# The last quarter of an MLP's first product by seven half-size products instead of eight

## The chip, the cores and the metric

One core of a Trainium2 chip runs the kernel. The metric is the device time of one execution in microseconds. Unless a profile is meant, it is the median of several executions. Engines: PE is TensorE (matmul), PEld its weight load, DVE VectorE, ACT ScalarE, POOL GpSimd, SP SyncE, which here only issues DMAs.

## The reference

One layer of a decoder in float32: 512 tokens, model width 1024. Two mixers (gated linear attention, GLA, and latent attention, MLA) work on the same normalised stream and are merged by gates; an MLP with squared ReLU follows. Each sub-layer ends in a residual sum and a layer norm.

```python
D_MODEL, SEQ, D_FF = 1024, 512, 4096
def layer(x):                                    # (512, 1024), float32
    h  = layer_norm(x, ln_in)
    h1 = layer_norm(alpha * h + token_mixer(h), ln1)      # GLA + MLA, gates, output product
    a  = jnp.square(jax.nn.relu(h1 @ w_ff1))              # (512, 4096): the product in question
    return layer_norm(alpha * h1 + a @ w_ff2, ln2)
```

The change is in `h1 @ w_ff1`, in its last 1024 of 4096 columns, and in what makes its operands ready.

## The kernel before

**Products in three terms.** TensorE's fast float32 form keeps fewer bits than float32, so each operand is held as a high part (a rounded copy) and a low part (the difference), and each product is three matmuls into the same bank: high·high, high·low, low·high. For weights, ACT makes the high part (`whi<-wraw`, L185) and DVE the low part (`wlo<-wraw,whi`, L186). Both have two buffers.

**The stream of weights.** All weights go through one list, `stream`, of 512 KB items in the order of use. `pump(i)` is called ahead of item i. It issues SP's DMAs up to two items ahead (into `wraw`, three buffers) and splits one item ahead. An item whose weights are a sum has no DMA of its own; it takes its source from the table `WQ` (tiles `wq`), and a "post" function may form the next sum from a raw item.

**The MLP in four chunks** of 1024 hidden columns (`ci` 0 to 3). In each, the first product is plain (`gemm_fm`, L238 to L240): a 128x128 weight block stays, 512 tokens stream, 8 blocks of columns x 8 inner blocks x 3 terms = 192 matmuls of 128x512. Its evacuation `ev_h` takes the ReLU on ACT (L1296) and the square. In the first three chunks the second product is done by `win_f2` with seven products in place of eight (the scheme below, list `WIN`, L1268 to L1270), whose results are copied by ACT into `ev` tiles (L1280) and added to the tiles `res` by accumulating POOL DMAs (L1282). In the last chunk the hidden tile is made differently: ACT squares into the high part (L1310), POOL squares again (L1311), DVE takes the low part (L1312), and the second product is plain (`f2last`, L271 to L273 and L1343 to L1345).

**Seven products.** A product of 2 x 2 blocks takes eight block products; with sums of the operands (Strassen's scheme in Winograd's form) it takes seven. The kernel before uses it in `gemm_unit` for 1024 gate columns, under the key "g1" (L1016 to L1018). Weights are named by quadrant, "11", "12", "21", "22", and sums t1 = 11 + 12, t2 = t1 + 22, t3 = 12 + 22, t4 = t2 + 21. The order of the products is 11, 21, t1, 22, t2, t3, t4 (list `FMO`). The matching sums of the activations come from `op_sums` (L965 to L972, then a split, L112). The results of the seven products are joined on DVE (L1025, L1033, L1036). An item there is two inner blocks by 512 columns, so each operand has two items of 24 matmuls of 128x256.

**What sets the order.** Work beside the matmuls is written as generators that `tick` advances between matmuls (`spawn`, `finish`). The program's order is then settled for each engine by a scheduler that simulates the kernel with its own costs; `tc.issue_after` adds an edge that it must respect.

Of the kernel before, what the change touches and what calls it, by code (L numbers as in the profile page):

```python
# [10 lines left out]
F32 = mybir.dt.float32  # L11
# [8 lines left out]
P = 128  # L20
# [32 lines left out]
def tile_hybrid_block(ctx: ExitStack, tc: tile.TileContext, I, out, dbg=None):  # L53
# [86 lines left out]
    st = {"dma": 0, "spl": 0, "gates": ()}  # L140
    DMA_AHEAD, SPLIT_AHEAD = 2, 1

    def plan(name, c0, n, k_lo=0, k_hi=None, heads=None, res=False, per=2):
# [17 lines left out]

    def pump(i):
        while st["dma"] < min(len(stream), i + 1 + DMA_AHEAD):
# [10 lines left out]
            e["raw"] = raw  # L174
        while st["spl"] < min(len(stream), i + 2 + SPLIT_AHEAD):
            e = stream[st["spl"]]
            if st["spl"] > i + e.get("ahead", SPLIT_AHEAD) and not e["res"]:
                break
            nk, n = e["nk"], e["n"]
            hi, lo = [A([P, nk, T * 2 // nk], F32R, w) for w in HOME["a" if e["res"] else e.get("home", "w")]]  # L180
            raw = e["src"]() if "src" in e else e.pop("raw")
            with ExitStack() as gates:
                for g in st["gates"]:
                    gates.enter_context(tc.issue_after(g.ins))
                st["ins"] = act(hi[:, :nk, :n], raw[:, :nk, :n], AF.Copy)  # L185
                vtt(lo[:, :nk, :n], raw[:, :nk, :n], f(hi[:, :nk, :n]), op=ALU.subtract)  # L186
# [120 lines left out]
    FMO = (("11", 0), ("21", 1), ("t1", 2), ("22", 5), ("t2", 3), ("t3", 6), ("t4", 4))  # L307
    UNITS = {"g1": ("w_in", C_G + D)}

# [6 lines left out]

    def u_src(key, i, j, hf):
# [4 lines left out]
    def u_sum(key, a, to, hf, x):  # L322
        t = WQ[key, (to, hf)] = WQ[key, (a, hf)]
        vtt(t, t, x, op=ALU.add)


    for key in UNITS:
        PL[key] = []
        for op, _ in FMO:
            for hf in range(2):  # L330
                PL[key].append(len(stream))
                e = {"nk": 2, "n": T, "res": False}
                if op[0] != "t":
                    e["dmas"] = [(slice(0, 2), u_src(key, int(op[0]) - 1, int(op[1]) - 1, hf), None)]
                else:
                    e["src"] = lambda q=(key, (op, hf)): WQ[q]
                if op == "22":
                    e["post"] = lambda raw, q=(key, "t1", "t2", hf): u_sum(*q, raw)
                elif op == "t2":
                    e["post"] = lambda raw, q=(key, "t2", "t4", hf): u_sum(*q, WQ[key, ("21", q[3])])  # L340
                stream.append(e)
    plan_qr(0)
    PL["yg", 0] = plan("w_o_gla", 0, T)
# [25 lines left out]
    FC = 4  # L369
    F1 = [((0, 4), (4, 2), (6, 2))] + [tuple((b, 2) for b in range(0, 8, 2))] * 2 + [((0, 4), (4, 4))]  # L370
    WIN = (("11", 0, 0), ("21", 0, 1), ("11", 1, 0), ("21", 1, 1), ("T1", 0, 2), ("T1", 1, 2), ("T2", 0, 3), ("T2", 1, 3),
           ("T4", 0, 4), ("T4", 1, 4), ("22", 0, 5), ("22", 1, 5), ("T3", 0, 6), ("T3", 1, 6))
    fb = 0
    for ci in range(FC):
        nb = 8
        for b, w in F1[ci]:
            PL["f1", ci, b] = plan("w_ff1", (fb + b) * P, w * P, res=(ci == 0 and b == 0), per=8 // w)
        if ci < FC - 1:
            plan_src(("f2", ci), [(op, hf) for op, hf, _ in WIN], HOMES)
        else:  # L380
            plan_zip("f2last", [("w_ff2", 0, fb, True), ("w_ff2", T, fb, True)])
        fb += nb
# [601 lines left out]

    def u_load(key, op):
        for hf in range(2):
            t = WQ[key, (op, hf)] = A([P, 2, T], F32, "wq")
            nc.sync.dma_start(t, u_src(key, *{"21": (1, 0)}.get(op, (0, 1)), hf))
            if op != "21":
                nc.gpsimd.dma_start(t, u_src(key, *{"t1": (0, 0), "t3": (1, 1)}[op], hf), accum_op=ALU.add)  # L990

    def gemm_unit(key, ops, evac, after=None):

        bank, e1, e5, u2 = {}, {}, {}, {}
        nk = 2
        for n, (op, ph) in enumerate(FMO):
            items = PL[key][2 * n:2 * n + 2]
            for g in range(2):
                bk = ("a" if ph in (0, 3, 6, 4) else "b", g)
                opens = ph in (0, 2, 1)  # L1000
                if opens:
                    bank[bk] = (PX if ph == 1 else MM)()
                o = bank[bk]
                for hf, it in enumerate(items):
                    pump(it)
                    hi, lo = stream[it]["w"]
                    for pp in range(nk):
                        while len(ops) <= nk * hf + pp:
                            tick(3)
                        xh, xl = ops[nk * hf + pp][ph]  # L1010
                        for a in range(2):
                            c = slice((2 * g + a) * P, (2 * g + a + 1) * P)
                            oa = o[:, a * 256:(a + 1) * 256]
                            first = opens and hf == 0 and pp == 0 and a == 0
                            last = hf == 4 // nk - 1 and pp == nk - 1
                            mm(oa, hi[:, pp, c], xh, start=first, stop=False, skip_group_check=True)  # L1016
                            mm(oa, hi[:, pp, c], xl, start=False, stop=False, skip_group_check=True)  # L1017
                            mm(oa, lo[:, pp, c], xh, start=False, stop=last, skip_group_check=True)  # L1018
                        if pp % 2:
                            tick(3)  # L1020
                if ph == 0:
                    e1[g] = B([P, T], F32, "e1")
                    act(e1[g], o, AF.Copy)
                elif ph == 1:
                    vtt(e1[g], o, e1[g], op=ALU.add)  # L1025
                    evac(0, 0, g, e1[g], None)
                elif ph == 2:
                    e5[g] = B([P, T], F32, "e5")
                    act(e5[g], o, AF.Copy)
                elif ph == 3:  # L1030
                    u2[g] = B([P, T], F32, "u2")
                    act(u2[g], o, AF.Copy)
                    vtt(u2[g], bank["b", g], u2[g], op=ALU.subtract)  # L1033
                    evac(1, 0, g, u2[g], None)
                elif ph == 6:
                    vtt(e5[g], e5[g], o, op=ALU.subtract)  # L1036
                    evac(1, 1, g, e5[g], None)
                elif ph == 4:
                    evac(0, 1, g, o, None)
            if after:  # L1040
                after(op)


# [208 lines left out]
    def win_f2(ci, hid):  # L1252
        bank = {}
        for n, (op, hf, ph) in enumerate(WIN):
# [21 lines left out]
            if hf == 1:  # L1276
                for t in range(2):
                    o = bank[{3: 0, 6: 0, 5: 2}.get(ph, ph), t]
                    e = B([P, T], F32, "ev")
                    st["ev"] = act(e, o, AF.Copy, scale=-1.0 if ph == 4 else 1.0)  # L1280
                    for tt, j in (((0, 0),), ((0, 0),), ((2, 1),), ((0, 1),), ((2, 0),), ((0, 1),), ((2, 0), (2, 1)))[ph]:
                        nc.gpsimd.dma_start(res[tt + t][:, j * T:(j + 1) * T], e, accum_op=ALU.add)  # L1282
            if n == 9 and ci + 1 < FC - 1:
                win_load(ci + 1)

    WT = {}
    for ci in range(FC):
        nb = 8
# [5 lines left out]
        def ev_h(a, ps):  # L1294
            r = B([P, T], F32, "relu")
            act(r, ps, AF.Relu)  # L1296
            if win:
                if a % 2 == 0:
                    hid.append({"R": A([P, 2, T], F32, "hr")})
                ops = hid[-1]  # L1300
                R = ops["R"]
                act(R[:, a % 2, :], r, AF.Square)
                if a % 2:
                    h1 = A([P, 2, 2, 256], F32R, "h1p")
                    split(R[:, :, :256], h1[:, 0], h1[:, 1])
                    ops[0], ops[1] = [(h1[:, 0, i], h1[:, 1, i]) for i in range(2)]
                    spawn(win_hid(R, ops))
                return
            hh = A([P, 2, T], F32R, "hid0")
            act(hh[:, 0, :], r, AF.Square)  # L1310
            gtt(r, r, r, op=ALU.mult)  # L1311
            vtt(hh[:, 1, :], r, f(hh[:, 0, :]), op=ALU.subtract)  # L1312
            hid.append(hh)
        for b, w in F1[ci]:
# [14 lines left out]
        else:  # L1329
            bg, bb = bcast_row("ln2_g"), bcast_row("ln2_b")  # L1330
            gemm_tm(PL["f2last"], hid, T, ev_res, tts=(0, 1))
# [67 lines left out]
```

## Time and profile before

| | us |
|---|---|
| median of 3 runs (lowest to highest) | 901.56 (900.95 to 901.74) |
| the profiled execution, its own time | 901.97 |
| its span in the trace | 900.2 |
| mean granted TensorE clock, share of full speed | 0.998 |
| TensorE busy, of the span | 880.9 (98%) |
| VectorE busy | 585.5 (65%) |
| ScalarE busy | 427.3 (47%) |
| GpSimd busy | 178.0 (20%) |
| last chunk's first product, on TensorE | 805.03 to 848.54 |
| gate unit "g1", on TensorE | 274.32 to 317.94 |

Times inside the kernel are counted from the start of the span. A row of a timeline gives start, duration, engine, line, operation, output<-inputs, shape, and in brackets the idle time of the engine just before it with what ended it. A row of a group gives count | busy time, mean ns of one | idle time before them. A matmul's duration reaches over the start of the next ones, since they are pipelined; its cost in a dense stretch is the distance between starts.

### The profile page before, as it was taken

How to read it: one execution, taken by the hardware profiler on the slowest of the kernel's cores; microseconds unless marked ns; L12 is line 12 of the kernel's file. 1: busy time of each engine (PE TensorE's matmuls, PEld its weight loads, DVE VectorE, ACT ScalarE, POOL GpSimd, SP SyncE). 2: the span in 40 equal slices, each digit the busy share in tenths (PEclk: the TensorE clock that was granted, in tenths of full speed). 3: DMA queues.
4: the chain of work that ended last, by engine and by line, in shares of the span. 5: the costliest groups of instructions: out<-in, count | busy, mean ns of one | idle time of the engine just before them, and what ended most of it. 6: DMA issues, size and time to landing. Idle time of an engine off the chain costs nothing.

```text
span 900.2 us, 12161 instructions
## 1 busy us (share of the span) xinstructions
PE 880.9 (98%) x4652; PEld 755.8 (84%) x4652; DVE 585.5 (65%) x953; ACT 427.3 (47%) x729; POOL 178.0 (20%) x196
## 2 busy tenths in 40 slices
PE   5999999999999999999999999999999999999996
PEld 5988888888889988888888888988888888888885
DVE  7835855577876645747756797997557646723565
ACT  5556443443546543445644423466367546733410
POOL 0103442444531010100000002104400520142200
PEclk9999999999999999999999999999999999999999
DMA  7414323216225623121207518005941990594311
GB/s 241 124 47 159 129 65 94 71 47 155 81 71 195 175 88 105 43 60 53 94 24 277 191 49 302 1 1 151 296 115 32 261 243 24 117 209 108 128 68 73
DMA packets 64776, 107.25 MB, mean 119 GB/s; under 512 B 7840, under 2 KB 27680, under 8 KB 64720
## 3 DMA queue, kind: packets, MB, share of 16 engines
q1 hardware_dynamic: 51344, 75.57, 26.3%
q0 software_dynamic: 11456, 27.27, 13.0%
q10 hardware_dynamic: 1920, 3.66, 1.2%
q8 instruction: 36, 0.59, 0.3%
q14 instruction: 20, 0.16, 0.1%
HBM read 89.18 MB, written 4.72 MB: 104 GB/s over the span
## 4 chain that ended last, share of the span: by engine, by line
PE 96%; DVE 2%; DMA 1%; ACT 1%; issue 0%; SPq 0%; DVEq 0%
PE mm L238 14%; PE mm L240 14%; PE mm L239 14%; PE mm L271 7%; PE mm L273 7%; PE mm L272 7%; PE px L1269 2%; PE px L1270 2%; PE px L1268 2%; PE px L723 2%; PE mm L1269 2%; PE mm L1270 2%; PE mm L1268 2%; PE mm L1018 1%; PE mm L1016 1%; PE mm L1017 1%
## 5 line engine op out<-in xcount | busy, mean ns | idle before, releaser
L186 DVE TENSOR_TENSOR wlo<-wraw,whi 128x1024 fp32r<-128x1024 f32 (+1 forms) x102 | 115.3, 1131 | 131.6 <-ACT whi L185 124.0
L185 ACT ACTIVATE whi<-wraw 128x1024 fp32r<-128x1024 f32 (+1 forms) x102 | 98.2, 962 | 109.5 <-PE mm L239 63.3
L238 PE MATMUL mm<-h,whi 128*128 128x512 f32 x352 | 137.6, 392 | 0.0
L239 PE MATMUL mm<-h,whi 128*128 128x512 f32 x352 | 137.3, 390 | 0.0
L240 PE MATMUL mm<-h,wlo 128*128 128x512 f32 x352 | 130.5, 390 | 0.0
L1282 POOL DMA_DIRECT2D res<-ev x48 | 42.1, 1018 | 187.5 <-ACT ev L1280 151.6
L238 PEld LDWEIGHTS mm<-h,whi 128*128 128x128 f32 x352 | 66.0, 188 | 13.5
L240 PEld LDWEIGHTS mm<-h,wlo 128*128 128x128 f32 x352 | 66.0, 188 | 13.5
L239 PEld LDWEIGHTS mm<-h,whi 128*128 128x128 f32 x352 | 66.1, 188 | 13.3
L272 PE MATMUL mm<-wlo,h 128*128 128x512 f32 x128 | 50.3, 393 | 0.0
L273 PE MATMUL mm<-whi,h 128*128 128x512 f32 x128 | 50.1, 392 | 0.0
L271 PE MATMUL mm<-whi,h 128*128 128x512 f32 x128 | 49.7, 403 | 0.0
L185 ACT ACTIVATE xh<-wraw 128x1024 fp32r<-128x1024 f32 (+1 forms) x28 | 27.1, 985 | 36.8 <-PE mm L273 16.5
L662 POOL TENSOR_TENSOR rp<-rp 128x256 f32<-128x256 f32 x32 | 31.6, 987 | 61.2 <-ACT E L667 44.8
L1296 ACT ACTIVATE relu<-mm 128x512 f32<-128x512 f32 x32 | 18.8, 595 | 49.3 <-PE mm L240 49.2
L186 DVE TENSOR_TENSOR wlo<-wq,whi 128x1024 fp32r<-128x1024 f32 x20 | 24.5, 1225 | 24.2 <-ACT whi L185 24.2
L391 POOL TENSOR_TENSOR mv<-mv,mhalf 128x1 f32<-128x1 f32 x4 | 4.6, 1154 | 172.4 <-DVE mv L390 172.4
L186 DVE TENSOR_TENSOR xl<-wraw,xh 128x1024 fp32r<-128x1024 f32 (+1 forms) x28 | 31.2, 1128 | 8.9 <-ACT xh L185 8.7
L669 DVE TENSOR_TENSOR M<-E,qk 128x512 f32<-128x512 f32 x32 | 27.8, 868 | 14.1 <-ACT E L667 14.1
L667 ACT ACTIVATE E<-rp 128x512 f32<-128x512 f32 x32 | 20.4, 638 | 24.9 <-POOL rp L663 24.9
L663 POOL TENSOR_TENSOR rp<-rp 128x256 f32<-128x256 f32 x32 | 28.2, 883 | 8.9 <-ACT q L692 6.7
L273 PEld LDWEIGHTS mm<-whi,h 128*128 128x128 f32 x128 | 24.0, 188 | 5.0
(405 smaller groups left out, 2415.3 us busy)
## 6 DMA issues: line engine op xcount, KB each, us to landing
wraw<-in_w_ff_dram SPq DMA_DIRECT2D x40, 512.0 KB, 4.5
wraw<-in_w_in_dram SPq DMA_DIRECT2D x38, 512.0 KB, 3.5
wq<-in_w_ff_dram POOLq DMA_DIRECT2D x24, 512.0 KB, 9.4
res<-ev POOLq DMA_DIRECT2D x48, 256.0 KB, 6.6
wraw<-in_w_o_gla_dram SPq DMA_DIRECT2D x8, 512.0 KB, 3.8
wraw<-in_w_o_mla_dram SPq DMA_DIRECT2D x8, 512.0 KB, 3.5
wraw<-in_w_out_dram SPq DMA_DIRECT2D x8, 512.0 KB, 3.9
wq<-in_w_in_dram SPq DMA_DIRECT2D x6, 512.0 KB, 5.5
```

Source lines behind the costliest of these rows:

```text
L185: st["ins"] = act(hi[:, :nk, :n], raw[:, :nk, :n], AF.Copy)
L186: vtt(lo[:, :nk, :n], raw[:, :nk, :n], f(hi[:, :nk, :n]), op=ALU.subtract)
L238: mm(o, hi[:, c], xh, start=first, stop=False)
L239: mm(o, hi[:, c], xl, start=False, stop=False)
L240: mm(o, lo[:, c], xh, start=False, stop=last)
L271: mm(o, xh, hi[:, :n], start=opens, stop=False, skip_group_check=share)
L272: mm(o, xh, lo[:, :n], start=False, stop=False, skip_group_check=share)
L273: mm(o, xl, hi[:, :n], start=False, stop=last, skip_group_check=share)
L1268: mm(o, xh[:, c], hi[:, pp], start=opens, stop=False, skip_group_check=True)
L1269: mm(o, xh[:, c], lo[:, pp], start=False, stop=False, skip_group_check=True)
L1270: mm(o, xl[:, c], hi[:, pp], start=False, stop=hf == 1 and pp == 1, skip_group_check=True)
L1282: nc.gpsimd.dma_start(res[tt + t][:, j * T:(j + 1) * T], e, accum_op=ALU.add)
```

## The change

1. The last chunk's first product goes through the seven-product unit, under the key "f1": 336 matmuls of 128x256 in place of 192 of 128x512.
2. A unit's item is now one operand by one group g of 256 columns: four inner blocks x 256 columns, for "g1" too. `unit` takes group after group, each with all its inner blocks.
3. The activations' sums for "f1" come from `op_sums` on `h1T`, spawned at step 10 of the second product of chunk 2. The weights 11 and 22 come through the stream; t1 is loaded by SP (quadrant 12) and POOL adds 11 by an accumulating DMA; 21 is loaded ahead into `wq` (`HELD`) at step 11. Quadrant 12 is loaded again after product 11, and t3 (12 + 22) is formed from it on DVE, as t2 and t4 are. The weight sums wait by `issue_after` for the last low part in the queue, and t3 and t4 are formed two items later (`later`).
4. The evacuation `ev_u` does ReLU, square and high-part copy on ACT and the low part on DVE; POOL's squares are gone. `Halves` gives the last product its hidden tiles by token half.
5. In chunk 2, from step 10 of `win_f2` on, the tiles that take the bank results come from the pool of the `T1` tiles in place of the `ev` buffers.
6. The two row loads for the last layer norm are issued after product t2.

```diff
@@ the weight stream
+            if "post2" in e:
+                later[st["spl"] + 2] = lambda p=e["post2"], r=raw: p(r)
+            later.pop(st["spl"], lambda: None)()
             st["spl"] += 1
...
+    HELD = (("21", "f1"),)
+    UNITS = {"g1": ("w_in", C_G + D), "f1": ("w_ff1", 3 * D)}
...
-        return src[:, 4 * hf + i:4 * hf + i + 3:2, c0 + j * T:c0 + (j + 1) * T]
+        c0 += j * T + g * 256
+        return src[:, i:8:2, c0:c0 + 256]
+
+    def u_sum(key, a, to, g, x, new=None):
+        src = WQ[key, (a, g)]
+        t = WQ[key, (to, g)] = src if new is None else new
+        with tc.issue_after(st["lo"].ins):
+            vtt(t, src, x, op=ALU.add)
...
+                if op == "22":
+                    e["post"] = lambda raw, q=(key, "t1", "t2", g): u_sum(*q, raw)
+                    if key == "f1":
+                        e["post2"] = lambda raw, q=(key, "12", "t3", g): u_sum(*q, raw)
                 elif op == "t2":
+                    e["post2" if key == "f1" else "post"] = lambda raw, q=(key, "t2", "t4", g): u_sum(*q, WQ[q[0], ("21", q[3])])
...
-    F1 = [((0, 4), (4, 2), (6, 2))] + [tuple((b, 2) for b in range(0, 8, 2))] * 2 + [((0, 4), (4, 4))]
+    F1 = [((0, 4), (4, 2), (6, 2))] + [tuple((b, 2) for b in range(0, 8, 2))] * 2 + [()]
...
@@ the unit: one operand, one group
+                o, it = bank[bk], PL[key, op, g]
+                pump(it)
+                hi, lo = stream[it]["w"]
+                for k in range(4):
...
+                    for a in range(2):
+                        c = slice(a * P, (a + 1) * P)
+                        oa = o[:, a * 256:(a + 1) * 256]
+                        mm(oa, hi[:, k, c], xh, start=opens and k == 0 and a == 0, stop=False, skip_group_check=True)
+                        mm(oa, hi[:, k, c], xl, start=False, stop=False, skip_group_check=True)
+                        mm(oa, lo[:, k, c], xh, start=False, stop=k == 3, skip_group_check=True)
...
@@ win_f2
-                    e = B([P, T], F32, "ev")
+                    if ci < FC - 2 or n < 10:
+                        e = B([P, T], F32, "ev")
+                    else:
+                        if t == 0:
+                            ev2 = A([P, 2, T], F32, "T1")
+                        e = ev2[:, t]
...
+            if ci == FC - 2 and n == U0:
+                t_h1.append(spawn(h1_sums()))
+            if ci == FC - 2 and n == U2:
+                fetch(PL["f1", "22", 0] + 1)
+            if ci == FC - 2 and n == U1:
+                u_load("f1", "t1")
+            if ci == FC - 2 and n == U3:
+                u_load("f1", "21")
...
+    U0, U1, U2, U3 = 10, 9, 9, 11
...
@@ evacuation of the last chunk
-            hh = A([P, 2, T], F32R, "hid0")
-            act(hh[:, 0, :], r, AF.Square)
-            gtt(r, r, r, op=ALU.mult)
-            vtt(hh[:, 1, :], r, f(hh[:, 0, :]), op=ALU.subtract)
-            hid.append(hh)
...
+            def ev_u(j, i, g, ps, sb):
+                def later():
+                    for _ in range(1 + 4 * i):
+                        yield
+                    r = ps if sb else B([P, T], F32, "relu")
+                    act(r, ps, AF.Relu)
+                    hh = A([P, 2, 2, 256], F32R, "hid0")
+                    act(r, r, AF.Square)
+                    act(hh[:, 0], r.rearrange("p (a c) -> p a c", a=2), AF.Copy)
+                    yield
+                    vtt(hh[:, 1], r.rearrange("p (a c) -> p a c", a=2), f(hh[:, 0]), op=ALU.subtract)
+                    hts[j, i, g] = hh
+                spawn(later())
...
+            def after1(op):
+                if op == "11":
+                    u_load("f1", "12")
+                if op == "t2":
+                    rows.extend(bcast_row(n) for n in ("ln2_g", "ln2_b"))
+            gemm_unit("f1", hops, ev_u, after1)
```

More of the change, by code (lines that the diff above doesn't have):

```diff
@@ L141, in tile_hybrid_block @@
     DMA_AHEAD, SPLIT_AHEAD = 2, 1
+    later = {}
     def plan(name, c0, n, k_lo=0, k_hi=None, heads=None, res=False, per=2):
@@ L983, in op_sums, with u_load @@
             ops.append(o)
[L985 to L992, printed above, removed]
+    def u_load(key, op, dma=nc.sync.dma_start):
+        for g in range(2):
+            t = WQ[key, (op, g)] = A([P, 4, 256], F32, "wq")
+            dma(t, u_src(key, *{"21": (1, 0)}.get(op, (0, 1)), g))
+            if op[0] == "t":
+                nc.gpsimd.dma_start(t, u_src(key, *{"t1": (0, 0), "t3": (1, 1)}[op], g), accum_op=ALU.add)
@@ L994, in gemm_unit, with unit, prod @@
+    def unit(key, ops, evac, after=None, pb=None):
         bank, e1, e5, u2 = {}, {}, {}, {}
-        nk = 2
-        for n, (op, ph) in enumerate(FMO):
-            items = PL[key][2 * n:2 * n + 2]
+        def prod(op):
+            ph = dict(FMO)[op]
+            opens = ph in (0, 2, 1)
             for g in range(2):
                 bk = ("a" if ph in (0, 3, 6, 4) else "b", g)
-                opens = ph in (0, 2, 1)
                 if opens:
[L1002 to L1020, printed above, removed]
```

96 lines of the change are left out of this document (60 added, 36 removed).

## The prediction

> **What bounds the kernel now.** I read the page's shares and its chain of waits first, then the timeline of TensorE around the two stages that the change touches, then busy time by stretch.
>
> ```profile
> PE 880.9 (98%) x4652; PEld 755.8 (84%) x4652; DVE 585.5 (65%) x953; ACT 427.3 (47%) x729; POOL 178.0 (20%) x196
> PE 96%; DVE 2%; DMA 1%; ACT 1%; issue 0%; SPq 0%; DVEq 0%
> ...
> 789.20:805.03 15.83, 15.83 (x72) 13.11 (x71) 3.68 (x3) 6.92 (x10) 6.06 (x7) 1.00 0.99 207
> 805.03:848.54 43.51, 43.51 (x193) 36.05 (x192) 14.64 (x12) 14.97 (x22) 8.61 (x8) 1.00 0.49 133
> 274.32:317.94 43.62, 43.14 (x358) 42.85 (x357) 28.00 (x31) 25.82 (x40) 3.45 (x3) 1.00 0.60 180
> 848.54:893.00 44.46, 43.99 (x217) 37.25 (x215) 30.81 (x46) 8.52 (x11) 8.15 (x7) 1.00 0.20 71
> ```
>
> The first two rows say that TensorE is busy for 98% of the span and carries 96% of the chain that ended last. The others are windows: length, busy time (instructions) of PE, PEld, DVE, ACT and POOL, granted clock, DMA share, GB/s. 805.03 to 848.54 is the product that the change rewrites, and TensorE has no idle time in it. 274.32 to 317.94 is the kernel's existing seven-product unit, for the gate columns ("g1"): the model for what comes. The clock is 1.00 in all. So what counts is TensorE's issue time, plus any wait that the denser schedule of the other engines puts into it.
>
> The spacing of two matmul widths, from the timeline (start, duration, which overlaps its neighbours):
>
> ```profile
> 848.09 0.39 PE L239 MATMUL mm<-h,whi 128*128 128x512 f32 x1
> 848.32 0.39 PE L240 MATMUL mm<-h,wlo 128*128 128x512 f32 x1
> 848.54 0.39 PE L271 MATMUL mm<-xh,hid 128*128 128x512 f32 x1
> ...
> 274.32 0.28 PE L1016 MATMUL mm<-h,whi 128*128 128x256 f32 x1
> 274.44 0.28 PE L1017 MATMUL mm<-h,whi 128*128 128x256 f32 x1
> 274.56 0.28 PE L1018 MATMUL mm<-h,wlo 128*128 128x256 f32 x1
> L238 PE MATMUL mm<-h,whi 128*128 128x512 f32 x64 | 24.9, 389 | 0.0
> ```
>
> The last row is one of three like it (L238 to L240) between 805 and 848.5: 192 matmuls in the plain product.
>
> **TensorE's own work.** Plain: 43.51 us over 192 is 0.2266 us each, which fits the 0.22 to 0.23 between starts. Seven-product: 7 products x 2 column groups x 4 inner blocks x 2 halves x 3 split terms = 336 matmuls of 128x256, at 0.120 us: 40.32 us. The difference is **-3.2 us**. It is less than the eighth that the scheme saves in columns (192 x 512 against 336 x 256), because a 256-wide matmul costs 0.120 and not half of 0.2266; the break-even spacing is 43.51/336 = 129.5 ns. The g1 window bears out the 0.120 for a whole unit: its PE busy time of 43.14 us holds 336 such matmuls and 22 others, 0.1205 us for a mean instruction.
>
> The Trainium skill ("TensorE: Matmul & The Clock Gate", section "Back-to-back issue gap") gives sustained spacings of about 81 ns for 128 columns and 131 ns for 512. By a straight line between them 256 columns would cost some 98 ns, an estimate, and the edit would run from 25.2 to 32.9 us, a loss of 7.7. The rows here, 0.22 to 0.23 and 0.12, disagree with it, and they decide.
>
> **Is the next weight always split in time?** A unit works through 14 items (7 operands x 2 groups) of 24 matmuls, 24 x 0.120 = 2.88 us. Each needs a high copy on ACT (L185), then a subtraction on DVE (L186), into two buffers, so that item i may be split only when item i-2 is read out.
>
> ```profile
> 302.42 0.28 PE L1017 MATMUL mm<-sh,whi 128*128 128x256 f32 x1
> 302.66 0.28 PE L1016 MATMUL mm<-sh,whi 128*128 128x256 f32 x1
> 302.74 1.06 ACT L185 ACTIVATE whi<-wq 128x1024 fp32r<-128x1024 f32 x1 [1.82 <-PE mm L1017]
> 303.84 1.23 DVE L186 TENSOR_TENSOR wlo<-wq,whi 128x1024 fp32r<-128x1024 f32 x1 [0.39 <-ACT whi L185]
> ...
> 312.29 0.38 PE L1018 MATMUL mm<-h,wlo 128*128 128x256 f32 x1 [0.48 <-DVE wlo L186]
> PE mm L1018 <- DVE wlo L186: 0.5, 1, 0.5
> ```
>
> The last high-part matmul of one item (302.42) ends at 302.70, the copy starts at 302.74, which is 0.08 after the next item's start (302.66), and the subtraction ends at 305.07, 2.41 after it. In the changed order the low part is wanted by the third matmul of the item after, at 2.88 + 0.24 = 3.12. Slack: **0.7 us per item**, less what DVE or ACT does in between. The last two rows show the only stall of the existing unit, 0.48 us once in 14 items (the waits view of TensorE from 274 to 318 has this row alone).
>
> What DVE has to do between 789.2, where it falls idle, and the product's end:
>
> ```profile
> L965 DVE TENSOR_TENSOR hraw<-h 128x512 f32<-128x512 f32 x8 | 6.2, 803 | 0.0
> L971 DVE TENSOR_TENSOR hx<-hraw,hx 128x256 f32<-128x256 f32 x4 | 1.7, 417 | 0.0
> L112 DVE TENSOR_TENSOR sh<-hx,sh 128x512 fp32r<-128x512 f32 x8 | 5.7, 740 | 3.1 <-ACT sh L111 3.1
> L324 DVE TENSOR_TENSOR wq<-wq,wq 128x1024 f32<-128x1024 f32 x2 | 2.5, 1225 | 0.1
> L1033 DVE TENSOR_TENSOR u<-mm,u 128x512 f32<-128x512 f32 x2 | 1.4, 688 | 0.1
> ...
> L186 DVE TENSOR_TENSOR wlo<-wraw,whi 128x1024 fp32r<-128x1024 f32 x6 | 7.3, 1223 | 16.4 <-ACT whi L185 16.4
> L1311 POOL TENSOR_TENSOR relu<-relu 128x512 f32<-128x512 f32 x4 | 5.1, 1293 | 18.8 <-ACT hid L1310 18.8
> L1312 DVE TENSOR_TENSOR hid<-relu,hid 128x512 fp32r<-128x512 f32 x4 | 5.1, 1312 | 4.3 <-POOL relu L1311 4.3
> ...
> 773.07 1.23 DVE L112 TENSOR_TENSOR xl<-hx,xh 128x1024 fp32r<-128x1024 f32 x1
> 774.21 1.22 DVE L186 TENSOR_TENSOR xl<-wq,xh 128x1024 fp32r<-128x1024 f32 x1
> 775.34 1.22 DVE L186 TENSOR_TENSOR wraw<-T,wraw 128x1024 fp32r<-128x1024 f32 x1
> ```
>
> Now: 3.68 + 14.64 = 18.3 us busy. Out: the plain product's eight splits (the six of the row and two before 805) of 1.223 = 9.8. In: fourteen splits, 17.1; the operand sums of h1, as for the gates (6.2, four lines like L971 of 1.7, 5.7) 18.7; six weight sums of 1.225 for t2, t3 and t4, 7.4; six bank combinations of 0.688, 4.1; the low parts of the hidden tiles stay. Sum 55.8 us, in 59.3 - 3.2 = 56.1 us. That looks full, but queued DVE instructions overlap: the last three rows start 1.13 and 1.14 apart and last 1.22. At 0.09 saved for each of some 60 instructions DVE is occupied for about 50 us, nine tenths. The schedule is tight and not impossible. I laid the compiled order of both engines against the item starts with these durations: the split of every item arrives, with 0.4 us to spare in the sixth and about 0.05 in the last, whose split stands behind weight sums. I allow **+0.5 us** of stalls for that, between 0 (as walked) and 13 times the 0.48 of the existing unit's one (6.2).
>
> The first items are prepared during the second product before it, where DVE is idle now:
>
> ```profile
> 795.09 1.22 DVE L186 TENSOR_TENSOR wlo<-wq,whi 128x1024 fp32r<-128x1024 f32 x1 [5.90 <-ACT whi L185]
> 803.60 1.23 DVE L186 TENSOR_TENSOR wlo<-wraw,whi 128x1024 fp32r<-128x1024 f32 x1 [4.21 <-ACT whi L185]
> ```
>
> The gaps in brackets (5.90 and 4.21 us) are where the h1 sums go; a sum just ahead of such a split delays it by at most 0.8 us, and these splits now finish some 3 us and more before their use.
>
> **Transfers.** The change loads quadrant 12 twice and 11 again, the latter by POOL accumulation into t1: 6 MB where 4 went. The critical ones are five SP loads of 512 KB issued between 786 and 789 (11 second group, 22 first, t1 second, 21 both), next to the POOL queue's result accumulations and t1's two accumulating loads, while the windows show a DMA share of 0.99.
>
> ```profile
> q0 software_dynamic: 1693, 5.14, 84.0%
> q1 hardware_dynamic: 1057, 1.06, 16.0%
> wraw<-in_w_ff_dram SPq DMA_DIRECT2D x3, 512.0 KB, 12.2
> ...
> q0 software_dynamic: 1772, 3.21, 69.0%
> q1 hardware_dynamic: 1088, 2.10, 24.4%
> wraw<-in_w_ff_dram SPq DMA_DIRECT2D x4, 512.0 KB, 4.2
> ```
>
> (Packets, MB, share; median us to landing; first from 701 to 722, then from 785 to 812.) Per packet SP's take 3.2 ns of 1 KB (16.0% of 21 us over 1057) and POOL's 10.5 ns (69.0% of 27 us over 1772). Taking packets in turn from both queues, in program order, the two loads of 21 land at about 804 and 807 and t1's second accumulation at about 809, where their splits start at 808.0, 810.9 and 816.6. Margin 3 to 8 us: cost nothing. The wait that this adds is POOL's second accumulation, held until its SP load has landed; behind it in POOL's queue stand the last result accumulations, whose sums the last product's evacuation reads 50 us later, and ACT's next copy into a tile that they free comes more than 5 us after. The Trainium skill ("DMA: Bandwidth & Descriptors", section "Queues, rings and completion order") says that an engine alternates between its queues by packet; the 1693 and 1057 packets of the crowded window fit roughly.
>
> **The rest.** The new g1 order (4 blocks x 256 columns an item) keeps 336 matmuls; its 0.48 stall may go, or another come: -0.5 to +0.5, I take **-0.2**. POOL's squares (1.293 each) leave; nobody on the path waited for them, and the ACT square and copy that replace them serve tiles that the last product reads at least 20 us later. The accumulation tiles from another pool end waits of ACT, not of TensorE. The two ACT-queue row loads move to a place with the DMA at about half load. Last product and tail stay.
>
> **Sum.** -3.2 + 0.5 - 0.2 = -2.9 us. The profiled execution took 901.97 us with a span of 900.2; its span becomes about 897.3. Against the median of 901.56, 0.4 below the profiled time, that is **898.6 us**. 0.2%, about what a measurement can tell from no change, is 1.8 us.
>
> **Rivals.**
> - *A few stalls eat the gain*, 1.1 to 4.7 us more of them than I allow: 899.8 to 903.3, within 0.2%. For it: the last item's 0.05 us of spare, and a DVE nine tenths full, so that one lateness passes on. Against: the g1 unit, with DVE busy for 28.00 of 43.62 us, lost only 0.48. Chance 0.16.
> - *DVE cannot keep up* (the slower side). If the sums stand before splits so that every item's low part comes late, the wait recurs on 13 items. To be 1.8 us slower it needs 5.0 us of stalls, 0.39 an item, so a chain 1.1 us longer than the rows give: about one weight sum (1.225) ahead of each split. At one in every item: 13 x (1.225 - 0.7) = 6.8 us, 905.2. Against: there are six such sums, not 13. Chance 0.07.
> - *21 or t1 lands late.* At the 50 GB/s that SP's queue had from 701 to 722 (1.06 MB in 21 us) the five loads, 2.6 MB, would take 52 us from 786, and TensorE would stop some 25 us: 924. It decides once 21 lands 5 us past 810.9. Against: that window's POOL queue carried 5.14 MB; here the second accumulation itself waits for its SP load. Chance 0.04.
> - *256-wide spacing not kept.* At 129.5 ns nothing is gained (901.6), at 140 it is 905. All rows of this width show 0.120, so 0.01.
>
> The main case has 0.72. So: faster 0.72, same 0.16, slower 0.12. The range leaves out the slower cases and the upper part of the stalls (12 and some 5 in 100): up to 902.0. Its low end has no stall at all and both g1 gains: 901.56 - 3.2 - 0.5 = 897.9, less 0.9 for the durations' rounding (0.120 to 0.0025 over 336): 897.0.
>
> **What would show it.** In the profile after, TensorE's block between the last 512-wide px matmul and the last product should last 40.3 to 41 us with 336 matmuls of 128x256 at 0.120 apart, its waits view should name DVE wlo for about half a microsecond, and no DMA wq. Wrong would be: waits on DVE wlo summing to over 1.5 us, a stop of several us on one of the 21 or t1 items (transfers), a gap at the start of the unit, or a last product that begins by waiting for hid.

## The result, and the profile after

| | before | after |
|---|---|---|
| median of 6 runs each, us (lowest to highest) | 901.65 (900.95 to 901.77) | 896.9 (896.5 to 897.46) |
| ratio, 95% interval | | 0.9949 (0.9936 to 0.9962) |
| the profiled execution, its own time, us | 901.97 | 896.5 |
| its span, us | 900.2 | 894.7 |

The change made the kernel 4.75 us faster. The prediction said faster, by 2.9 us, 898.6 with a range from 897.0; the measured median is 0.1 us under that range.

The page of the kernel after, shares of the span and chain of waits:

```profile
PE 877.5 (98%) x4796; PEld 760.5 (85%) x4796; DVE 614.5 (69%) x1003; ACT 445.1 (50%) x757; POOL 170.4 (19%) x190
PE 97%; DVE 1%; DMA 1%; ACT 0%; issue 0%; DVEq 0%
```

Its windows (start:end, length, busy us and instructions of PE, PEld, DVE, ACT and POOL, granted clock, DMA share, GB/s), for the gate unit, the stretch ahead of the last chunk's first product, that product, and the last product:

```profile
273.14:316.16 43.02, 43.02 (x359) 42.82 (x358) 28.36 (x31) 25.47 (x40) 3.63 (x3) 1.00 0.65 182
787.40:803.24 15.84, 15.84 (x71) 13.12 (x70) 15.19 (x27) 10.26 (x17) 6.99 (x8) 1.00 1.10 242
803.24:843.62 40.38, 40.38 (x338) 40.35 (x337) 34.36 (x40) 28.57 (x42) 5.04 (x6) 1.00 0.67 170
843.62:888.00 44.38, 44.02 (x218) 37.25 (x216) 29.22 (x47) 9.67 (x13) 2.78 (x3) 1.00 0.28 95
```

The gate unit takes 43.02 us (43.62 before) and is busy throughout. The last chunk's first product takes 40.38 us (43.51 before), also without idle time: 336 matmuls at 0.120 us are 40.32. The DMA share is 1.10 from 787 to 803 (0.99 in the matching stretch before), and VectorE's 15.19 us there stand where it had 3.68.

The end of the unit on TensorE's timeline (line numbers are those of each kernel's own file):

```profile
843.38 0.28 PE L1029 MATMUL mm<-h,whi 128*128 128x256 f32 x1
843.50 0.28 PE L1030 MATMUL mm<-h,wlo 128*128 128x256 f32 x1
843.62 0.40 PE L278 MATMUL mm<-xh,hid 128*128 128x512 f32 x1
```

The whole waits view of TensorE (waited for: us in total, times, longest):

```profile
PE px L421 <- ACT x L410: 8.3, 1, 8.3
PE px L738 <- DVE SD L694: 0.5, 1, 0.5
PE mm L247 <- DVE wlo L190: 0.5, 1, 0.5
PE mm L278 <- ACT h L424: 0.4, 1, 0.4
PE mm L245 <- ACT h L424: 0.3, 1, 0.3
```

No unit line (L1028 to L1030) waits for anything, in the new unit or in the gate unit, whose 0.48 us wait is gone. What is left are waits elsewhere. The kernel before had them too, but for the 0.4 us at L278, which comes at 11.6 us, near the start.

VectorE's timeline in the tight part of the unit, in the kernel after:

```profile
827.50 1.23 DVE L190 TENSOR_TENSOR wlo<-wq,whi 128x1024 fp32r<-128x1024 f32 x1 [0.52 <-ACT whi L189]
828.64 1.22 DVE L335 TENSOR_TENSOR wq<-wq,wraw 128x1024 f32<-128x1024 f32 x1
830.38 1.22 DVE L190 TENSOR_TENSOR wlo<-wq,whi 128x1024 fp32r<-128x1024 f32 x1 [0.52 <-ACT whi L189]
831.52 1.22 DVE L335 TENSOR_TENSOR wq<-wq,wq 128x1024 f32<-128x1024 f32 x1
...
839.12 1.23 DVE L190 TENSOR_TENSOR wlo<-wq,whi 128x1024 fp32r<-128x1024 f32 x1
```

Split, sum, half a microsecond idle, and again, every 2.88 us. The last split ends at 840.35; the last item starts at 843.62 - 2.88 = 840.74 and wants its low part at 840.98, with its third matmul. The spare there is 0.6 us.

From stage to stage the two traces differ by 0.6 us in the gate unit, 3.1 in the last chunk's first product, 1.2 ahead of TensorE's first matmul (9.47 against 8.29) and 0.6 behind its last one (7.66 against 7.09): 5.5 us, the difference of the spans.

### The profile page after: what moved, and what is told of

The parts are those of the page before. It is cut to its first block, busy times and chain, and to the rows that moved or that the text cites. A ratio compares the mean times of both kernels' runs of the same rounds, so it can differ in the third digit from the quotient of the medians.

```text
span 894.7 us, 12542 instructions
## 1 busy us (share of the span) xinstructions
PE 877.5 (98%) x4796; PEld 760.5 (85%) x4796; DVE 614.5 (69%) x1003; ACT 445.1 (50%) x757; POOL 170.4 (19%) x190
## 4 chain that ended last, share of the span: by engine, by line
PE 97%; DVE 1%; DMA 1%; ACT 0%; issue 0%; DVEq 0%
PE mm L245 12%; PE mm L247 12%; PE mm L246 12%; PE mm L278 7%; PE mm L279 7%; PE mm L280 7%; PE mm L1030 3%; PE mm L1029 3%; PE mm L1028 3%; PE px L1288 2%; PE px L1287 2%; PE px L1286 2%; PE px L738 2%; PE mm L1288 2%; PE mm L1287 2%; PE mm L1286 2%
## 5 line engine op out<-in xcount | busy, mean ns | idle before, releaser
L190 DVE TENSOR_TENSOR wlo<-wraw,whi 128x1024 fp32r<-128x1024 f32 (+1 forms) x98 | 110.4, 1127 | 110.0 <-ACT whi L189 102.4
L245 PE MATMUL mm<-h,whi 128*128 128x512 f32 x288 | 112.7, 392 | 0.0
L246 PE MATMUL mm<-h,whi 128*128 128x512 f32 x288 | 112.4, 390 | 0.0
L247 PE MATMUL mm<-h,wlo 128*128 128x512 f32 x288 | 107.1, 390 | 0.0
L245 PEld LDWEIGHTS mm<-h,whi 128*128 128x128 f32 x288 | 54.0, 188 | 11.0
L246 PEld LDWEIGHTS mm<-h,whi 128*128 128x128 f32 x288 | 54.1, 188 | 10.8
L247 PEld LDWEIGHTS mm<-h,wlo 128*128 128x128 f32 x288 | 53.9, 188 | 11.0
L190 DVE TENSOR_TENSOR wlo<-wq,whi 128x1024 fp32r<-128x1024 f32 x30 | 36.7, 1225 | 19.4 <-ACT whi L189 19.4
L278 PE MATMUL mm<-whi,h 128*128 128x512 f32 x128 | 49.7, 403 | 0.0
L677 POOL TENSOR_TENSOR rp<-rp 128x256 f32<-128x256 f32 x32 | 31.6, 988 | 61.1 <-ACT E L682 44.8
L189 ACT ACTIVATE whi<-wq 128x1024 fp32r<-128x1024 f32 x30 | 31.7, 1058 | 19.7 <-PE mm L1029 11.4
L1028 PE MATMUL mm<-sh,whi 128*128 128x256 f32 x128 | 36.2, 283 | 0.0
L1029 PE MATMUL mm<-sh,whi 128*128 128x256 f32 x128 | 36.2, 283 | 0.0
L1030 PE MATMUL mm<-sh,wlo 128*128 128x256 f32 x128 | 36.2, 283 | 0.0
```

Of the source, the lines that this page charges most:

```text
L190: st["lo"] = vtt(lo[:, :nk, :n], raw[:, :nk, :n], f(hi[:, :nk, :n]), op=ALU.subtract)
L245: mm(o, hi[:, c], xh, start=first, stop=False)
L246: mm(o, hi[:, c], xl, start=False, stop=False)
L247: mm(o, lo[:, c], xh, start=False, stop=last)
L278: mm(o, xh, hi[:, :n], start=opens, stop=False, skip_group_check=share)
L1028: mm(oa, hi[:, k, c], xh, start=opens and k == 0 and a == 0, stop=False, skip_group_check=True)
```

## The experiments

### The parts, each by itself, and the ends of the execution

The kernels before and after, once more unchanged:

> The kernel before, unchanged, for a second trace of it. Between the two traces at hand the span shrank by 5.5 us: 3.1 in the last chunk's first product, 0.6 in the gate unit, 1.2 before TensorE's first matmul and 0.6 after its last one; the medians differ by 4.75. Theory A (the ends are chance: landing times of the first loads and the close of the execution vary from run to run): the time from the start to the first matmul and from the last matmul to the end of the span differ here from the first trace's 9.5 and 7.7 us by some tenths up to 1 us. Theory B (the ends belong to the program): they are the first trace's again within 0.1 us. Both: the same time within 0.1%.

> The changed kernel, unchanged, for a second trace. Theory A: its first matmul starts anywhere between 8.2 and 9.6 us, and its ends overlap with those of the kernel before. Theory B: 8.3 us to the first matmul and 7.1 us after the last again, and a time 4.6 to 4.9 us below before. Both: the first product of the last chunk lasts 40.4 us and the gate unit 43.0, without a TensorE wait in either.

The gate unit's new layout alone, with the loads and the order that go with it (in the kernel before; one line shown for the whole edit, comments added here), and the new product with the old gate unit:

```diff
 # in the kernel before
-    e = {"nk": 2, "n": T, "res": False}          # gate unit: two inner blocks x 512 columns an item
+    e = {"nk": 4, "n": 256, "res": False}        # four inner blocks x 256 columns, group after group
```

> The kernel before with the new item layout and order in the gate unit alone (four inner blocks by 256 columns an item); the last chunk's first product stays plain. Theory A: the gate unit is 0.5 to 0.6 us shorter (its one wait on a low part, 0.48 us, is gone) and nothing else moves: 901.0, 0.9994 of before. Theory B: 0.6 to 1.6 us faster, with part of the missing microsecond of the ends in it.

```diff
 # in the kernel after
-    gemm_unit("g1", hops, ev_gate, after)
+    gemm_unit0("g1", hops, ev_gate, after)       # layout, loads and order of the kernel before
```

> The changed kernel with the gate unit's layout and order as before; the last chunk's first product goes through the new unit. Theory A: the product takes 40.4 us against 43.5, the gate unit keeps its 0.48 us wait: 898.5, 3.1 us below before. Theory B: with the missing microsecond, 897.5.

The two small edits alone, in the kernel before:

```diff
-            act(hh[:, 0, :], r, AF.Square)
-            gtt(r, r, r, op=ALU.mult)
+            act(r, r, AF.Square)
+            act(hh[:, 0, :], r, AF.Copy)
...
+                        if t == 0:
+                            ev2 = A([P, 2, T], F32, "T1")
+                        e = ev2[:, t]
```

> The kernel before with only the two small edits: the square and the high-part copy on ACT in place of POOL's square, and the last bank results of chunk 2 in tiles from the other pool; the plain product and the old gate unit stay. The prediction priced both at nothing, since nobody on TensorE's path waited for POOL's squares or those copies: 901.6, the time before within 0.1%. Rival (they are worth by themselves part of the 7.2 and 4.4 us that their removal from the changed kernel cost): 1 us or more faster. For the ends, which shrank by about 1 us in the changed kernel: if they go with these edits, the first matmul starts below 9.0 us or the tail is 7.1; if not, 9.2 to 9.5 and 7.7.

| kernel | median us | ratio to before (95%) | first matmul at | last matmul to end | between, us |
|---|---|---|---|---|---|
| before, first trace | 901.65 | | 9.47 | 7.66 | 883.07 |
| before again | 901.52 | 0.9999 (0.9991 to 1.0008) | 9.21 | 7.66 | 883.15 |
| two small edits alone | 901.61 | 1.0 (0.9991 to 1.0009) | 9.15 | 7.66 | 883.06 |
| gate layout alone | 901.0 | 0.9993 (0.9984 to 1.0002) | 9.22 | 7.98 | 882.09 |
| new product, old gate unit | 898.05 | 0.9964 (0.9951 to 0.9978) | 8.34 | 7.72 | 879.78 |
| after, first trace | 896.9 | 0.9949 (0.9936 to 0.9962) | 8.29 | 7.09 | 879.35 |
| after again | 896.89 | 0.9948 (0.9935 to 0.996) | 8.78 | 7.05 | 879.29 |

The parts come out about as sized: the gate unit is worth -0.6 in the median (an interval that still touches no change; its trace has -1.0 between the first and the last matmul and 0.3 more behind them), the new product -3.3 us between the first and the last matmul, both together -3.8, and the small edits by themselves nothing. The ends are not chance, or not only. The tail repeats within 0.05 us in both kernels, 7.66 and 7.05 to 7.09, although its instructions are the same. The traces say where it differs. In all fourteen the last store is issued 4.1 us after the last matmul and has landed 6.1 to 6.2 us after it. What follows, the semaphores and drains that close the execution, takes 0.9 us in the nine traces with both parts, 1.5 to 1.6 us in the two of the kernel before, with the small edits alone and with the new product alone, and 1.8 us with the gate layout alone. So this part of the gain lies behind all of the kernel's work, and neither part alone brings it. Over all traces of this study the first matmul starts between 8.27 and 9.0 us in the ten with the new product and between 9.15 and 9.47 in the four without. The first instructions are the same too; what differs is when the third load of x lands (7.4, 7.1 and 6.2, 6.7 us in the traces of before and after). Why it does, and why the closing is shorter, was not found. About 1 us of the gain sits in these ends, outside the code that was changed.

### The edits that the prediction costed at nothing, taken back one by one

Results into `ev` buffers again; POOL's squares again; the third weight sum by POOL's accumulating load, as the gate unit has it. (The prediction put the first two at nothing; the third it counted as VectorE's time alone, two of the six weight sums.) All in the kernel after:

```diff
-                    if ci < FC - 2 or n < 10:
+                    if True:
                         e = B([P, T], F32, "ev")
```

> The changed kernel, but the last bank results of chunk 2 go into ev buffers again in place of tiles from the other pool. The prediction's reading (these tiles end waits of ACT, none of TensorE): the same time. Rival, from the trace after: the unit's first two bank copies on ACT then take buffers that are free only when two of POOL's result accumulations have landed, which happens there at 812.96 and 815.08; the copies stand at 807.2 and 810.1 on ACT, and the high parts of the fourth and fifth item stand behind them. The fourth's low part, wanted at 812.1, comes at about 816: TensorE waits some 4 us there and up to 1 us on the next item, 4 to 5 us slower than the changed kernel.

```diff
-                    act(r, r, AF.Square)
-                    act(hh[:, 0], r.rearrange("p (a c) -> p a c", a=2), AF.Copy)
+                    act(hh[:, 0], r.rearrange("p (a c) -> p a c", a=2), AF.Square)
+                    gtt(r, r, r, op=ALU.mult)
```

> The changed kernel with POOL's squares back in the evacuation (ACT squares into the high part, POOL squares in place, DVE takes the low part). The prediction costed this edit at nothing: the same time as the changed kernel within 0.3 us. Rival: DVE's low part now waits about 0.7 us longer for POOL than for ACT's copy, eight times, and the weight splits stand behind it on DVE; with about 0.6 us of slack an item that could cost 0 to 2 us.

```diff
-                        e["post2"] = lambda raw, q=(key, "12", "t3", g): u_sum(*q, raw)
...
-                    u_load("f1", "12")
+                    u_load("f1", "t3")
```

> The changed kernel with the third weight sum formed by an accumulating POOL load of quadrant 22 on top of quadrant 12, as the gate unit does, in place of VectorE. DVE loses two instructions of 1.22 us, the queues gain 1 MB. Theory (no engine but TensorE counts while everything arrives in time): same as the changed kernel within 0.3 us; the two accumulations can land at about 827 and 831 and their items are split at about 829 and 832. Rival: the second one comes late and TensorE waits 1 to 3 us once.

| in the kernel after | median us | ratio to before (95%) | against 896.9 |
|---|---|---|---|
| `ev` buffers | 901.28 | 1.0002 (0.9986 to 1.0017) | +4.4 |
| POOL's squares | 904.14 | 1.0021 (1.0012 to 1.003) | +7.2 |
| third sum by POOL's load | 900.42 | 0.9984 (0.9975 to 0.9992) | +3.5 |

These kernels scatter more than the kernel after: their runs go from 898.46 to 906.03, from 901.19 to 905.02 and from 899.35 to 901.51, against 896.5 to 897.46. So the sizes are medians, and each trace below is one execution. Each of the three by itself is worth more than the 3.1 us that the new product saves on TensorE, though the first two, both together, were worth nothing in the kernel before. They are what keeps TensorE fed.

With POOL's squares, TensorE's waits view has one new row:

```profile
PE mm L1030 <- DVE wlo L190: 4.7, 1, 4.7
```

VectorE's waits view in the unit names POOL, where it had no wait for POOL in the kernel after:

```profile
DVE hid L1387 <- POOL e L1385: 4.4, 1, 4.4
```

VectorE's timeline there:

```profile
820.05 1.52 DVE L1387 TENSOR_TENSOR hid<-e,hid 128x512 fp32r<-128x512 f32 x1 [4.38 <-POOL e L1385]
821.49 1.21 DVE L190 TENSOR_TENSOR wlo<-wq,whi 128x1024 fp32r<-128x1024 f32 x1
```

VectorE stands 4.4 us at the low part of the first hidden tile, with the next weight's split (821.49) behind it. POOL's timeline, to see why its square is so late:

```profile
814.47 1.74 POOL L1305 DMA_DIRECT2D res<-T  x2 [8.21 <-ACT hid L1384]
817.21 1.74 POOL L1305 DMA_DIRECT2D res<-T  x2 [0.99 <-ACT hid L1384]
818.32 2.69 POOL L1385 TENSOR_TENSOR e<-e 128x512 f32<-128x512 f32 x2
```

The square's input was ready at 814.2 (ACT's square ran from 813.59 for 0.63). Ahead of it in POOL's queue stand result accumulations. The releaser in brackets is ACT, which had long been done or has nothing to do with them. The first pair starts 0.5 us behind the landing, at 813.9, of an earlier accumulation for which it waits. The one for which the second pair waits landed at 815.8, so the rest of that pair's 0.99 us of idle time is not explained. The expectation had the place right (VectorE behind POOL) and the size wrong, 0 to 2 us, since it counted POOL's arithmetic and not POOL's queue.

A second cost came with the wait. TensorE's timeline after it:

```profile
822.75 0.44 PE L1030 MATMUL mm<-sh,wlo 128*128 128x256 f32 x1 [4.70 <-DVE wlo L190]
822.99 0.41 PE L1028 MATMUL mm<-sh,whi 128*128 128x256 f32 x1
823.20 0.42 PE L1029 MATMUL mm<-sh,whi 128*128 128x256 f32 x1
```

And two windows of the same kernel:

```profile
823.00:828.00 5.00, 5.00 (x31) 5.00 (x31) 2.57 (x3) 0.93 (x1) 0.00 (x0) 0.66 0.41 82
828.00:838.00 10.00, 10.00 (x85) 10.00 (x85) 8.23 (x8) 4.28 (x6) 0.00 (x0) 1.00 0.19 63
```

The starts are 0.21 us apart in place of 0.120, and the granted clock of the next five microseconds is 0.66: some seventeen matmuls at 0.213 us, 1.6 us on top of the wait. Wait and slow clock, 6.3 us, are nearly all of the 6.5 us by which this trace's span exceeds that of the kernel after (901.2 against 894.7).

With the `ev` buffers the total is near what the rival said, the place is not. ACT's waits view from 780 to 820 (2.2 us was its longest such wait in the kernel after):

```profile
ACT ev L1303 <- DMA res<-ev: 5.5, 3, 4.5
```

VectorE's timeline in that run:

```profile
793.28 1.22 DVE L190 TENSOR_TENSOR xl<-wq,xh 128x1024 fp32r<-128x1024 f32 x1 [5.52 <-ACT xh L189]
794.42 1.29 DVE L980 TENSOR_TENSOR hraw<-h,h 128x512 f32<-128x512 f32 x2
```

And the longest of TensorE's waits, on its timeline:

```profile
813.76 0.39 PE L1030 MATMUL px<-h,wlo 128*128 128x256 f32 x1 [1.99 <-DVE wlo L190]
```

A bank copy on ACT stands 4.5 us for a result accumulation; a high-part copy stands behind it, VectorE behind that, and the activations' sums begin at 794.42 where the kernel after has them at 789.02. From there TensorE waits 0.7, 0.3 and 2.0 us for low parts, and after the last of them the clock falls again (0.213 us between starts for 3 us). That only the buffers were changed does not mean that only the wait moved: the order of ACT's instructions changed with them.

With the third sum by POOL, ACT's waits view in the unit:

```profile
ACT whi L189 <- DMA wq<-in_w_ff_dram: 6.6, 2, 5.5
```

and TensorE's:

```profile
PE mm L1026 <- ACT u L1042: 2.3, 1, 2.3
```

Quadrant 12's second group lands at 827.4 here, which the accumulation that follows it must wait for; the two sums are there at 832.9 and 835.6, not at 827 and 831. The bank copy that TensorE names stands behind the late high part on ACT. So the sum on VectorE spares no work, it spares a second trip through a queue that is full.

### The transfers

```diff
-    U0, U1, U2, U3 = 10, 9, 9, 11
+    U0, U1, U2, U3 = 10, 9, 9, 13
```

> The changed kernel with the two loads of quadrant 21 issued two steps of the second product later (about 795 in place of 786 and 787). In the trace after they landed at 800.4 and 805.6, 14.6 and 18.5 us after their issue, behind 22 and t1 in the same queue. Theory (the queue was full anyway, so issue time is not what counts): they land within 2 us of that, ahead of the splits at 806.3 and 809.1 or at most 1 us late; 0 to 1 us slower. Rival (they land as long after their issue as before): 809 and 814, TensorE waits about 3 us on one and 2 more on the other, 3 to 5 us slower.

897.13 us, 0.9948 (0.9935 to 0.9962): the kernel after, within its runs. The view of queues and loads from 783 to 810 in the kernel after (packets, MB, share; KB of one, median us from issue to landing):

```profile
q0 software_dynamic: 1967, 2.71, 58.1%
q1 hardware_dynamic: 3190, 3.21, 44.0%
wq<-in_w_ff_dram SPq DMA_DIRECT2D x5, 512.0 KB, 18.5
```

The same five loads in the run with the late issue:

```profile
wq<-in_w_ff_dram SPq DMA_DIRECT2D x5, 512.0 KB, 13.8
```

Issued 6 to 7 us later, the two loads landed at 802.4 and 807.2 against 800.4 and 805.6. They stand in a queue either way, and the time of issue did not matter here.

### How much room VectorE has

An extra subtraction of half a tile, or of the whole one, ahead of each low part of the unit:

```diff
+                if e.get("unit") == "f1":
+                    vtt(lo[:, :2, :n], raw[:, :2, :n], f(hi[:, :2, :n]), op=ALU.subtract)   # or :4
                 st["lo"] = vtt(lo[:, :nk, :n], raw[:, :nk, :n], f(hi[:, :nk, :n]), op=ALU.subtract)
```

> The changed kernel, but in the last chunk's unit each low part is made with an extra subtraction of half the tile just ahead of the whole one (0.6 us more on DVE in each of 14 chains). Chain theory (slack of 0.6 to 0.7 us per item, and nothing adds up): 0 to 0.5 us slower. Queue theory (DVE is the limit when full: the trace after shows it idle for some 6 us in the unit, and 12 of the extra pieces, 7.2 us, fall into it): 1 to 3 us slower, the waits in the second half of the unit, where the weight sums and evacuations are.

> As the kernel before this one with the whole subtraction done twice (1.14 us more of DVE time in each chain). Chain theory, as the prediction priced its slower rival: 13 x (1.14 - 0.7) = 5.7 us slower than the changed kernel, spread evenly over the items. Queue theory: 12 x 1.14 = 13.7 us of work against 6 us of idle time, 7 to 8 us slower, and the waits stand where DVE has sums and evacuations in its queue.

| in the kernel after | median us | ratio to before (95%) | against 896.9 |
|---|---|---|---|
| half a subtraction more | 902.21 | 1.0007 (0.9998 to 1.0016) | +5.3 |
| a whole one more | 907.0 | 1.0062 (1.0046 to 1.0079) | +10.1 |

Both theories were too low. With the half dose TensorE's waits view reads:

```profile
PE mm L281 <- DVE xl L192: 1.3, 1, 1.3
PE mm L1032 <- DVE wlo L192: 1.1, 3, 0.5
PE px L1032 <- DVE wlo L192: 0.6, 2, 0.4
```

and the window of the unit:

```profile
803.75:849.80 46.05, 43.03 (x330) 40.86 (x329) 44.51 (x55) 33.00 (x47) 4.93 (x6) 1.00 0.64 170
```

VectorE is busy for 44.51 of 46.05 us: its queue is full, and what does not fit comes out behind the unit, where the last product waits for its first split (xl). The 10.1 us of the whole dose agree with 14 x 1.14 = 16 us of work less the 6 that were idle. The same sum for the half dose, 14 x 0.6 = 8.4 less 6, gives 2.4 us where 5.3 were measured, so it does not hold in general, and the agreement may be luck. Part of the gap lies in the view of waits: its rows add up to 3.0 us, while the time between the first and the last matmul grew by 4.9. The doses are not clean either, since the schedule was settled anew with them and mixed the unit's last matmuls with those of the last product. What they show is that VectorE has little room to spare, not how much a given piece of work costs. The clock stayed at 1.00 here: no wait was over 1.5 us.

One more, meant to begin the activations' sums two steps later:

> The changed kernel with the activation sums begun two steps of the second product later, some 5.4 us; nothing else is edited. In the run with the ev buffers, one wait of 4.5 us on ACT put the same sums 5.4 us later and the unit stalled. Theory (VectorE's queue has about 6 us to spare over the whole stretch but almost none before the fourth item; sums begun late are late for good): TensorE waits 2 to 4 us on low parts in the first four items, 3 to 5 us slower than the changed kernel, the slower if one wait is over 2 us, since after such waits TensorE's matmuls took 0.213 in place of 0.120 us for some 3 us. Rival (the order among the engines mattered there, not the lateness): within 1 us of the changed kernel.

896.42 us, 0.9943 (0.993 to 0.9957), and the first sum on VectorE starts at 788.91, where it was (789.02). The scheduler put it back into the same gap, so the run tells nothing on the theory; it serves as a third measurement of the kernel after (8.29 to the first matmul, 7.05 behind the last).

## Why the prediction was right, and where it was not

- **Bound and main term.** Right. TensorE's issue time sets the time, and -3.2 us for the product was -3.1 (43.51 to 40.38). The spacing of 0.120 us, taken from the gate unit, held for all 336 matmuls. The rival of a wider spacing is out.
- **Stalls in the unit.** The allowance of +0.5 was not needed: there is none. The walk through VectorE's queue was right in kind: its busy time from 787 to 844 is 15.19 + 34.36 = 49.6 us, where about 50 were forecast. Its spare time in the last item is 0.6 us and not 0.05.
- **Gate unit.** -0.2 taken, -0.6 measured: the wait of 0.48 went, as the lower bound had it.
- **Ends.** The step that failed is the sentence "Last product and tail stay". The instructions did stay; the ends still shrank by about 1 us in the median, 0.6 behind the last matmul (1.5 to 0.9 us for the closing of the execution) and, from trace to trace of the two kernels, 0.4 to 1.2 ahead of the first. Together with the two terms above, 0.5 + 0.4 + about 1, less 0.1 for the product and 0.1 for the new median of before, this is the 1.7 us between 898.6 and 896.9, and it puts the median just under the range. The cause of the ends is open; that the sign and the main term came out right does not rest on them.
- **Transfers.** Right: landing times were forecast at 804 and 807 on the clock of before for the loads of 21 and 809 for t1's second accumulation; shifted by the 1.8 us that the trace after runs ahead there, they came at 802.2, 807.4 and 812.2, the last 3 us later than forecast and still 4 ahead of its use. The late-issue run shows the margin. The packets of the window (1967 and 3190) are not one to one, and neither are the 1693 and 1057 that the prediction took for a rough fit. POOL's triggers stood still for 4.7 us there, behind a load; whether that is the cause was not tested. The Trainium skill's rule of alternating packets ("DMA: Bandwidth & Descriptors", "Queues, rings and completion order") gives the landing times here well enough; it was not tested by itself.
- **"Nobody on the path waited for them."** True of the kernel before, as the run with the small edits alone shows (901.61), and the sum came out right for it. But the prediction named no price for the case that the edits were missing, and that price is 4.4 and 7.2 us, and 3.5 for the third sum. They are not decoration beside the seven products: with any one of them left out the change would have been worth 1.2 us at most, or a loss of 2.5.
- **The slower rival.** VectorE that can't keep up was the right mechanism to fear. Priced at 6.8 us for one weight sum an item, it measured 10.1 with a whole subtraction more, and it set in much earlier than at a chain 1.1 us longer: 0.6 us an item already cost 5.3. The prediction weighed each chain by its own slack, with nothing added up from item to item; in these runs VectorE's whole queue was full (busy for 44.51 of 46.05 us with the half dose).

## What to carry to other kernels

Here a stage that trades matmul time for work on other engines paid only while the queues beside TensorE stayed free of foreign waits. Look for what stands ahead of a feeding instruction in its own queue (a DMA trigger that waits, a copy into a buffer that a DMA still reads), and not only for how long it takes. An edit that is worth nothing in the old schedule may be what the new one stands on, so price it by taking it out of the new kernel. In the full queue of this stage, issuing two loads 6 to 7 us earlier bought nothing, while a transfer that had to follow another one cost its whole second trip (822.2 to 832.9, and 827.9 to 835.6).

## What the runs showed of the hardware

After a wait of 2.0 us or more in a dense stretch TensorE ran at a lower granted clock for about 3 us: 0.213 us between 256-wide matmuls in place of 0.120, after waits of 2.0, 2.3 and 4.7 us, which adds 1.2 to 1.6 us. After waits of up to 1.5 us in the runs with extra subtractions it did not. What decides between the two was not measured. A window of the run with `ev` buffers, from the matmul behind its 2.0 us wait on:

```profile
813.80:817.40 3.60, 3.60 (x18) 3.60 (x19) 2.24 (x3) 0.92 (x2) 0.37 (x1) 0.53 1.11 264
```

A window of the run with half a subtraction more, behind its 1.3 us wait:

```profile
843.60:848.60 5.00, 4.98 (x33) 4.58 (x34) 5.00 (x6) 4.83 (x8) 0.00 (x0) 1.00 0.38 131
```

The granted clock is 0.53 in the first and 1.00 in the second. The Trainium skill ("TensorE: Matmul & The Clock Gate", "Part 1: The HAM clock gate (the "warmup" mystery)") has a half-rate clock after about 3.4 us of idle time; the half rate agrees, the 3.4 us do not, as 2.0 us were enough here.

The time from the last matmul to the end repeats to a few hundredths of a microsecond within one program and differs by up to 0.9 us between programs with the same last instructions (7.05 to 7.98). The difference lies behind the landing of the last store: 0.9 us from there to the end in the kernel after, 1.5 us in the kernel before, 1.8 us with the gate layout alone.
